# A decoder block on one core: a fourth pair of split buffers in its woven stretch, half-size raw weights, and tiles moved by 128 bytes

## The chip, the core and the metric

The kernel runs on 1 core of one Trainium2 chip. The metric is device time of one execution in microseconds (us), the median of several runs. A second, profiled execution gives the trace: engines PE (TensorE, with its weight loads as PEld), DVE (VectorE), ACT (ScalarE), POOL (GpSimd) and SP, whose queue issues most of the transfers. Times in a trace count from the first instruction; L368 is line 368 of the kernel.

## What is computed

One layer of a decoder for 256 tokens of 2048 features, in float32. The projections are split into heads, go through a sparse attention and a retention, and come together in two gated branches and an MLP:

```python
h = rms_norm(x, ln1_g[l])
proj = h @ w_in[l]
aq, ak, av, iq, ik, iw, rq, rk, rv, rg, ga, gb = jnp.split(proj, offsets, axis=-1)
...
o_attn = dsa_attention(aq, ak, av, iq, ik, iw, topk)
...
y_ret = retention_chunkwise(rq, rk, rv, log_gamma)
o_ret = jax.nn.silu(rg) * group_norm_heads(y_ret, ret_gn_g[l], ret_gn_b[l])
merged = jax.nn.sigmoid(ga) * (o_attn @ w_up_attn[l]) + jax.nn.sigmoid(gb) * (o_ret @ w_up_ret[l])
x = x + merged @ w_out[l]
h2 = rms_norm(x, ln2_g[l])
x = x + jnp.square(jax.nn.relu(h2 @ w_ff1[l])) @ w_ff2[l]
```

## The kernel before

Every large product is made of three products in a reduced-precision type. A raw weight tile (128 partitions, KC = 4 slices of 512 columns, 1 MB) is loaded by SP; half of it (HC = 2 slices) is an **item**. For each item `split_now` has ACT write the high part `whi` (L367) and DVE the low part `wlo` = raw - whi (L368). TensorE then makes three products per slice and 128 tokens: high times high, high times low, low times high (L420 to L422). The activations are split in the same way; they are the stationary operands: `act` (the normed input hT, and oT of the attention), later `xf`.

The list `program()` holds all items in the order in which TensorE uses them. `weights` takes the next item, and `ahead` first emits what lies before it: loads of items up to LOAD_AHEAD = 8 further on, as far as `room` allows, and splits of items up to SPLIT_AHEAD = 2 further on. The pairs `whi`, `wlo` come from the pool `wp`, three of each. So the split of item i+3 writes over the pair of item i, and waits until TensorE has done with it. In the last part of the kernel (from L911 on) a pool `f1` holds a fourth pair, for every item whose number leaves 3 by 4, and splits then go three items ahead.

The **woven stretch** is the list `gates()`. It weaves two kinds of items. *Quarter items* belong to the two gates GA and GB, four units in all; each unit is a Strassen-like scheme of 7 products with 4 items each, and a quarter item has 2 slices for 128 tokens, so 6 products, which go to one of three PSUM banks `pq`. Some of these products use sums of two quarter tiles, which DVE adds in place (`total`, L357, put behind the split of an item that GATE_SUMS names); for these products TensorE's stationary operands are `act` for three of the seven and forms `hx` for four. The forms are differences of the normed input's quarters, made by ACT and DVE at the start of the stretch (`h_forms`, L717 to L732). *Plain items* belong to ten ordinary blocks (`BESIDE`: the rest of RV, UA, RQ, RK); each has 2 slices for 256 tokens, so 12 products, into banks `pm`. 112 quarter items and 80 plain ones alternate, about 7 to 5: two plain items never follow each other, two quarter items sometimes do. In this stretch splits are emitted with a higher priority than the rest (L344), and a scheduler orders each engine's instructions by it.

Raw tiles of quarter items lie in a ring of six (four in `rp`, two in the pool `cx`). Raw tiles of plain items lie in `rawc`, a ring of two whole tiles in the pool `px` (L757, L313); a tile may be requested when both halves of the tile two before it are split (`room`, L377). SP's queue issues the loads in order, each waiting for the instruction that frees its place.

Pools with `side="right"` are laid out from the top of each partition downwards, one below the other: `rp`, `sp` (with n_sm = 25 small buffers of 32 bytes), `px`, then `ep` or `cx`. `hx`, 32 KB per partition, lies at the bottom of `cx`.

Of the kernel before, what the change touches and what calls it, by code (L numbers as in the profile page):

```python
# [10 lines left out]
F32 = mybir.dt.float32  # L11
# [6 lines left out]
P = 128  # L18
# [4 lines left out]
BN = 512  # L23
# [9 lines left out]
KC, HC = 4, 2  # L33
FG = 8
NG = DFF // (FG * P)
# [90 lines left out]
BESIDE = [("RV", 2), ("RV", 3)] + [("UA", i) for i in range(4)] + [(z, i) for z in ("RQ", "RK") for i in range(2)]  # L126
# [20 lines left out]
def program():  # L147

    out = [(z, h, s) for h in range(DK // KC) for s in range(KC // HC) for z in (("AK", 0), ("I", 0))]
    for key in [("I", 1), ("I", 2), ("AV", 0)] + [("AQ", i) for i in range(4)] + [("RV", 0), ("RV", 1)]:  # L150
        out += block(key)
    out += gates()
    for i in range(4):
        out += block(("RG", i))
    out += [(z, h, s) for h in range(DK // KC) for s in range(KC // HC) for z in (("UR", 0), ("UR", 1))]
    for key in [("UR", 2), ("UR", 3)] + [("O", i) for i in range(4)] + [("F1", i) for i in (1, 0)]:
        out += block(key)
    for g in range(1, NG):
        out += merged(g)
    return out + [("F2", NG - 1, i, h, s) for i in range(D // BN) for h in F2_HALVES for s in range(KC // HC)]  # L160
# [17 lines left out]
def block_kernel(ctx, tc, cst, rot, xt, gains, w, x, ret_gn_g, ret_gn_b, out):  # L178
# [5 lines left out]
    wp = ctx.enter_context(tc.tile_pool(name="wp", bufs=1))  # L184
    rp = ctx.enter_context(tc.tile_pool(name="rp", bufs=1, side="right"))
    sp = ctx.enter_context(tc.tile_pool(name="sp", bufs=1, side="right"))
    px = ctx.enter_context(tc.tile_pool(name="px", bufs=1, side="right"))
    ap = [ctx.enter_context(tc.tile_pool(name="a0", bufs=1)), tc.alloc_tile_pool(name="a1", bufs=1, reuse_waits="tile")]
    ep = tc.alloc_tile_pool(name="ep", bufs=1, side="right", reuse_waits="tile")
    dp = ctx.enter_context(tc.tile_pool(name="dp", bufs=1, space=bass.MemoryType.DRAM))  # L190
    W_NORM, W_SOFT, W_GN = 3, 5, 7
    n_stg, n_mid, n_sm = 8, 11, 25
    uid = [0]
    late = {"mid": ep}

    def nm(s):
        uid[0] += 1
        return f"{s}_{uid[0]}"
# [65 lines left out]

    at, B, off = {}, {}, 0
    for key, name, _, nk, _, n in stream():
        B[key] = (nk, n)
        for h in range(nk // KC):  # L270
            at[key, h] = (w[off:off + KC * P * n].rearrange("(p c n) -> p c n", p=P, c=KC), n)
            off += KC * P * n
    use = program()

    def tile_of(item):
        if item[0] == "Q":
            return (PRODUCTS[ORDER[item[2]]][1], item[1], item[3]), 0
        if item[0] == "F2":
            return item[:4], 0
        return item[0], item[1]  # L280

    def sum_of(item):

# [14 lines left out]
    raws, parts = {}, {}  # L298
    next_load, next_split, now, quarter, second_w, n_second = [0], [0], [0], [0], [0], [0]

    def ring(key):
        return key in BESIDE or (key[0] == "F2" and key[1] < NG - 1)

    LOAD_AHEAD, SPLIT_AHEAD, AHEAD = 8, 2, 60
    HT = KC // HC

    XROWS = (3, 5, 6, 7)

    def load(i):
        key = loads[i]  # L310
        src, n = at[key]
        if ring(key[0]):
            r = raws[key] = late["rawc"][:, second_w[0] % 2]  # L313
            second_w[0] += 1
        else:
            pool, tag, bufs = rp, "raw", 4
            if key[0][0] in QUARTERS:
                quarter[0] += 1
                if (quarter[0] - 1) % 6 >= 4:
                    pool, tag, bufs = late["f2"], "rawb", 2  # L320
            r = raws[key] = pool.tile([P, KC, BN], F32, tag=tag, name=nm("raw"), bufs=bufs)
        if i >= 2 * DK // KC:
            nc.sync.dma_start(r[:, :, :n], src)
        elif i % 2:

            for c0, c in ((0, 1), (1, 1), (2, 2)) if i == 1 else ((0, 2), (2, 2)):
                k = i // 2 * KC + c0
                nc.sync.dma_start(xts[:, k:k + c, :], xt[:, k:k + c, :])
                for z in loads[i - 1:i + 1]:
                    src, n = at[z]  # L330
                    if (i, z, c) != (1, key, 1):
                        nc.sync.dma_start(raws[z][:, c0:c0 + c, :n], src[:, c0:c0 + c, :])
                    elif c0:
                        nc.sync.dma_start(raws[z][:, :2, :n], src[:, :2, :])
        if i in XROWS:
            for j, z in list(enumerate(xsb))[XROWS.index(i) * 2:][:2]:
                nc.sync.dma_start(z, x[j // 4 * P:(j // 4 + 1) * P, j % 4 * BN:(j % 4 + 1) * BN])

    first_gate = use.index(("Q", GATES[0], 0, 0, 0))
    last_gate = len(use) - 1 - use[::-1].index(("Q", GATES[-1], len(ORDER) - 1, HK // KC - 1, HT - 1))  # L340

    def split(i):
        if first_gate - 16 <= i <= last_gate:
            with tc.high_priority(offset=AHEAD):  # L344
                split_now(i)
        else:
            split_now(i)

    def split_now(i):
        item = use[i]  # L350
        key, h = tile_of(item), item[-1]
        raw, n = raws[key], at[key][1]
        early = sum_of(item) and item[1] not in GATES

        def total():
            one, two = (raws[z] for z in sum_of(item))
            nc.vector.tensor_tensor(one, one, two, op=ALU.add)  # L357

        if early:
            total()  # L360
        pool, bufs = (late["f1"], 1) if "f1" in late and i % 4 == 3 else (wp, 3)
        hi = pool.tile([P, HC, BN], F32R, tag="whi", name=nm("whi"), bufs=bufs)
        lo = pool.tile([P, HC, BN], F32R, tag="wlo", name=nm("wlo"), bufs=bufs)
        for c0, nk in ((0, 1), (1, 1)) if i < 4 else ((0, HC),):
            src = raw[:, h * HC + c0:h * HC + c0 + nk, :n]
            a, b = hi[:, c0:c0 + nk, :n], lo[:, c0:c0 + nk, :n]
            nc.scalar.activation(a, src, AF.Copy)  # L367
            nc.vector.tensor_tensor(b, src, a.bitcast(F32), op=ALU.subtract)  # L368
        if sum_of(item) and not early:
            total()  # L370
        parts[i] = (hi, lo)

    def room(i):
        key = loads[i][0]
        if key[0] in QUARTERS and "f2" not in late:
            return False
        return not ring(key) or ("rawc" in late and second_w[0] - n_second[0] // HT < 2)  # L377

    def ahead(i):
        for _ in range(2):  # L380
            while next_load[0] < len(loads) and first_use[next_load[0]] <= i + LOAD_AHEAD and room(next_load[0]):
                load(next_load[0])
                next_load[0] += 1
            while next_split[0] < min(len(use), i + SPLIT_AHEAD + ("f1" in late) + 1):
                n_second[0] += ring(tile_of(use[next_split[0]])[0])
                split(next_split[0])
                next_split[0] += 1

# [270 lines left out]
    def strassen(item):  # L659
# [11 lines left out]
        for c in range(HC):  # L671
            products([b[to]], (ws[0][:, c], ws[1][:, c]), [form(PRODUCTS[p][0], h * KC + s * HC + c)], own and c == 0,
                     (h, s, c) == (HK // KC - 1, HT - 1, HC - 1), True)
        if (h, s) != (HK // KC - 1, HT - 1):
            return
# [68 lines left out]
    for i in range(2):  # L744
        ps = run_block(("RV", i), of(hT))
        for t in range(T):
            keep("rv", t, i, evicted(ps[t], t))
        if i == 0:
            drain()
            deal(pm=4, pq=3, pt=1)  # L750
            ep.release()
            cx = late["f2"] = tc.alloc_tile_pool(name="cx", bufs=1, side="right", reuse_waits="tile")
            hx = cx.tile([P, 2, 4, HK, P], F32R, tag="hx", name="hx")
            raw = [cx.tile([P, HK, S], F32, tag="rawb", name=nm("xr"), bufs=2) for _ in range(2)]
            for j, z in enumerate(raw):
                nc.sync.dma_start(z, xt[:, j * HK:(j + 1) * HK, :])
            late["rawc"] = px.tile([P, 2, KC, BN], F32, tag="big2", name="rawc")  # L757
            work.append(h_forms(raw))
    drain()

# [37 lines left out]
                work.append(rotated(evicted(ps[t], t), t, int(key == "RK"), i, rkT if key == "RK" else rqT))  # L798

    cx.release()  # L800
    del late["f2"], late["rawc"]
    deal(pm=4, pt=2, pa=2)
    ap[1] = tc.alloc_tile_pool(name="a2", bufs=1, reuse_waits="tile")
    rT = act_pair(1)
# [1 line left out]
    n_mid = 7  # L806
# [216 lines left out]
    def second(item):  # L1023
# [11 lines left out]
        order = [(c, slice(0, T)) for c in range(HC)]  # L1035
        if (g, i, h, s) == (NG - 1, D // BN - 1, F2_HALVES[-1], HT - 1):
            order = [(c, slice(t, t + 1)) for t in range(T) for c in range(HC)]
        for c, tt in order:
            k = h * KC + s * HC + c
            products(ps[tt], (ws[0][:, c], ws[1][:, c]), [of(hid)(g % 2 * FG + k, t) for t in range(T)][tt],  # L1040
                     (h, s, c) == (F2_HALVES[0], 0, 0), (h, s, c) == (F2_HALVES[-1], HT - 1, HC - 1))
        if (h, s) == (F2_HALVES[-1], HT - 1):
# [58 lines left out]
```

## Time and profile before

| What | Value |
|---|---|
| Median of 3 runs | 1631.78 us (1631.16 to 1632.28) |
| The profiled execution | 1630.73 us |
| Its span, first to last instruction | 1629.0 us |
| Granted TensorE clock | 1.000 |
| PE, DVE, ACT busy in the span | 1616.6, 1268.6, 1000.1 us |
| Bytes moved by the DMA engines | 353.88 MB |
| The woven stretch on PE | from 272.98 to 658.47 us |

In a row of a timeline the columns are start in us, duration in us, engine, line, operation, output and inputs, sizes; a bracket gives the engine's idle time before it and what ended it. In a row of waits they are who waited for whom, us in total, how often, and the longest. Rows that group instructions end with busy us, mean ns of one, and the idle time before them. A row of a window has its stretch, its length, then for PE, PEld, DVE, ACT and POOL the busy us and the number of instructions, then the granted clock, the share of the DMA engines and GB/s. A product's duration in the trace (0.39 us) overlaps the next one; the distance from start to start is its cost.

### The profile page before, as it was taken

How to read it: one execution, taken by the hardware profiler on the slowest of the kernel's cores; microseconds unless marked ns; L12 is line 12 of the kernel's file. 1: busy time of each engine (PE TensorE's matmuls, PEld its weight loads, DVE VectorE, ACT ScalarE, POOL GpSimd, SP SyncE). 2: the span in 40 equal slices, each digit the busy share in tenths (PEclk: the TensorE clock that was granted, in tenths of full speed). 3: DMA queues.
4: the chain of work that ended last, by engine and by line, in shares of the span. 5: the costliest groups of instructions: out<-in, count | busy, mean ns of one | idle time of the engine just before them, and what ended most of it. 6: DMA issues, size and time to landing. Idle time of an engine off the chain costs nothing.

```text
span 1629.0 us, 19406 instructions
## 1 busy us (share of the span) xinstructions
PE 1616.6 (99%) x7366; PEld 1330.7 (82%) x7366; DVE 1268.6 (78%) x1307; ACT 1000.1 (61%) x1238; POOL 100.4 (6%) x141
## 2 busy tenths in 40 slices
PE   9999999999999999999999999999999999999998
PEld 8977787777778877888888878888888888888887
DVE  6577676978787998677765488898989898989884
ACT  7555567565566666444444576667767676767672
POOL 0000000000000000010100000000000000000000
PEclk9999999999999999999999999999999999999999
DMA  9635337665666744754777564767677777777583
GB/s 332 220 140 181 130 141 272 248 225 186 229 235 259 256 176 165 254 171 174 255 251 261 193 246 164 252 212 237 220 232 233 232 233 232 233 222 230 169 252 135
DMA packets 68206, 353.88 MB, mean 217 GB/s; under 512 B 7696, under 2 KB 14480, under 8 KB 31888
## 3 DMA queue, kind: packets, MB, share of 16 engines
q1 hardware_dynamic: 51616, 311.32, 51.7%
q0 software_dynamic: 13760, 35.14, 9.8%
q10 hardware_dynamic: 2736, 6.18, 1.0%
q8 instruction: 58, 0.95, 0.2%
q14 instruction: 36, 0.29, 0.1%
HBM read 325.34 MB, written 27.26 MB: 216 GB/s over the span
## 4 chain that ended last, share of the span: by engine, by line
PE 92%; DVE 4%; ACT 2%; issue 1%; DMA 0%; POOL 0%; DVEq 0%; POOLq 0%; ACTq 0%
PE pm L421 14%; PE pm L422 14%; PE pm L420 14%; PE pq L421 8%; PE pq L422 8%; PE pq L420 8%; PE pf L420 7%; PE pf L422 7%; PE pf L421 7%; DVE wlo L368 2%; PE pt L449 1%; ACT whi L367 1%; DVE raw L357 1%; PE pa L647 1%; PE pa L620 1%
## 5 line engine op out<-in xcount | busy, mean ns | idle before, releaser
L368 DVE TENSOR_TENSOR wlo<-raw,whi 128x1024 fp32r<-128x1024 f32 (+2 forms) x528 | 627.5, 1200 | 244.9 <-ACT whi L367 238.5
L367 ACT ACTIVATE whi<-raw 128x1024 fp32r<-128x1024 f32 (+2 forms) x528 | 546.9, 1042 | 403.1 <-PE pm L422 262.7
L420 PE MATMUL pm<-whi,act 128*128 128x512 f32 (+1 forms) x1056 | 414.4, 395 | 2.4 <-ACT whi L367 2.4
L421 PE MATMUL pm<-wlo,act 128*128 128x512 f32 (+1 forms) x1056 | 407.3, 386 | 2.0 <-DVE wlo L368 2.0
L422 PE MATMUL pm<-whi,act 128*128 128x512 f32 (+1 forms) x1056 | 407.3, 386 | 0.0
L368 DVE TENSOR_TENSOR wlo<-rawc,whi 128x1024 fp32r<-128x1024 f32 x192 | 234.5, 1221 | 50.9 <-ACT whi L367 49.3
L367 ACT ACTIVATE whi<-rawc 128x1024 fp32r<-128x1024 f32 x192 | 203.5, 1060 | 103.1 <-PE pm L422 44.4
L421 PEld LDWEIGHTS pm<-wlo,act 128*128 128x128 f32 x1056 | 198.5, 188 | 43.6 <-DVE wlo L368 6.1
L420 PEld LDWEIGHTS pm<-whi,act 128*128 128x128 f32 x1056 | 198.4, 188 | 43.4 <-ACT whi L367 4.6
L422 PEld LDWEIGHTS pm<-whi,act 128*128 128x128 f32 x1056 | 198.3, 188 | 37.7
L357 DVE TENSOR_TENSOR raw<-raw,raw 128x2048 f32<-128x2048 f32 x88 | 201.2, 2286 | 0.8
L420 PE MATMUL pf<-whi,act 128*128 128x512 f32 x512 | 200.0, 391 | 0.0
L421 PE MATMUL pf<-wlo,act 128*128 128x512 f32 x512 | 199.4, 389 | 0.0
L422 PE MATMUL pf<-whi,act 128*128 128x512 f32 x512 | 199.4, 389 | 0.0
L420 PE MATMUL pq<-whi,xf 128*128 128x512 f32 x392 | 154.3, 394 | 0.0
L422 PE MATMUL pq<-whi,xf 128*128 128x512 f32 x392 | 152.7, 390 | 0.0
L421 PE MATMUL pq<-wlo,xf 128*128 128x512 f32 x392 | 152.6, 389 | 0.0
L422 PEld LDWEIGHTS pf<-whi,act 128*128 128x128 f32 x512 | 96.1, 188 | 20.1
L420 PEld LDWEIGHTS pf<-whi,act 128*128 128x128 f32 x512 | 96.0, 188 | 20.0 <-ACT whi L367 0.4
L421 PEld LDWEIGHTS pf<-wlo,act 128*128 128x128 f32 x512 | 96.2, 188 | 19.8
L422 PEld LDWEIGHTS pq<-whi,xf 128*128 128x128 f32 x392 | 73.6, 188 | 15.5
L421 PEld LDWEIGHTS pq<-wlo,xf 128*128 128x128 f32 x392 | 73.7, 188 | 14.7
(166 smaller groups left out, 1419.9 us busy)
## 6 DMA issues: line engine op xcount, KB each, us to landing
raw<-in_w_dram SPq DMA_DIRECT2D x180, 1024.0 KB, 5.8
rawc<-in_w_dram SPq DMA_DIRECT2D x96, 1024.0 KB, 5.5
sums<-ev POOLq DMA_DIRECT2D x56, 256.0 KB, 5.4
raw<-in_w_dram SPq DMA_DIRECT2D x8, 736.0 KB, 4.6
raw<-in_w_dram SPq DMA_DIRECT2D x7, 512.0 KB, 7.4
raw<-in_w_dram SPq DMA_DIRECT2D x8, 368.0 KB, 7.7
stg<-in_x_dram SPq DMA_DIRECT2D x8, 256.0 KB, 7.5
rv<-stg POOLq DMA_DIRECT2D x8, 256.0 KB, 4.6
```

Source lines behind the costliest of these rows:

```text
L357: nc.vector.tensor_tensor(one, one, two, op=ALU.add)
L367: nc.scalar.activation(a, src, AF.Copy)
L368: nc.vector.tensor_tensor(b, src, a.bitcast(F32), op=ALU.subtract)
L420: nc.tensor.matmul(d, h, hi, start=first, stop=False, skip_group_check=skip)
L421: nc.tensor.matmul(d, h, lo, start=False, stop=False, skip_group_check=skip)
L422: nc.tensor.matmul(d, l, hi, start=False, stop=last, skip_group_check=skip)
L449: nc.tensor.transpose(ps[:, c * P:(c + 1) * P], src[:, c * P:(c + 1) * P], ident)
L620: nc.tensor.matmul(ps[:, a * n:(a + 1) * n], qT[:, h0 + a, :], kT[:, j, :n], start=True, stop=True)
L647: nc.tensor.matmul(po, vv[:, c, j * HD:(j + 1) * HD], pT, start=(c == 0), stop=(c == t))
```

## The change

Four things are changed, all for the woven stretch.

- The pool `cx` gets a fourth pair `whi`, `wlo`, used for every item whose number leaves 3 by 4, and in the stretch splits go three items ahead.
- Raw weights of plain items are loaded in halves of 512 KB, one for each item, into a ring of three halves, which now lies in `cx`.
- The pool `px` is released before the stretch and made anew behind it (as `px2`), so that `cx` may use its place.
- n_sm grows from 25 to 29. The four small buffers more take 128 bytes, and all pools of the right side below them begin 128 bytes lower.

```diff
-    px = ctx.enter_context(tc.tile_pool(name="px", bufs=1, side="right"))
+    px = tc.alloc_tile_pool(name="px", bufs=1, side="right", reuse_waits="tile")
...
-    n_stg, n_mid, n_sm = 8, 11, 25
+    n_stg, n_mid, n_sm = 8, 11, 29
...
-            at[key, h] = (w[off:off + KC * P * n].rearrange("(p c n) -> p c n", p=P, c=KC), n)
+            src = w[off:off + KC * P * n].rearrange("(p c n) -> p c n", p=P, c=KC)
+            if key in BESIDE:
+                for i in range(HT):
+                    at[key, h, i] = (src[:, i * HC:(i + 1) * HC], n)
+            else:
+                at[key, h] = (src, n)
...
-        return item[0], item[1]
+        return item if item[0] in BESIDE else item[:2]
...
     def ring(key):
-        return key in BESIDE or (key[0] == "F2" and key[1] < NG - 1)
+        if key in BESIDE:
+            return 3
+        return 2 if key[0] == "F2" and key[1] < NG - 1 else 0
...
-            r = raws[key] = late["rawc"][:, second_w[0] % 2]
+            r = raws[key] = late["rawc"][:, second_w[0] % ring(key[0])]
...
-        key, h = tile_of(item), item[-1]
+        key, h = tile_of(item), 0 if item[0] in BESIDE else item[-1]
...
         pool, bufs = (late["f1"], 1) if "f1" in late and i % 4 == 3 else (wp, 3)
+        if "fourth" in late and i % 4 == 3:
+            pool, bufs = late["fourth"], 1
...
-        return not ring(key) or ("rawc" in late and second_w[0] - n_second[0] // HT < 2)
+        n = ring(key)
+        return not n or ("rawc" in late and second_w[0] - (n_second[0] // HT if key[0] == "F2" else n_second[0]) < n)
...
-            while next_split[0] < min(len(use), i + SPLIT_AHEAD + ("f1" in late) + 1):
-                n_second[0] += ring(tile_of(use[next_split[0]])[0])
+            while next_split[0] < min(len(use), i + SPLIT_AHEAD + ("f1" in late or "fourth" in late) + 1):
+                n_second[0] += ring(tile_of(use[next_split[0]])[0]) > 0
...
             ep.release()
+            px.release()
...
-            late["rawc"] = px.tile([P, 2, KC, BN], F32, tag="big2", name="rawc")
+            late["rawc"] = cx.tile([P, 3, HC, BN], F32, tag="rawc", name="rawc")
+            late["fourth"] = cx
...
-    del late["f2"], late["rawc"]
+    del late["f2"], late["rawc"], late["fourth"]
+    second_w[0] = n_second[0] = 0
+    px = ctx.enter_context(tc.tile_pool(name="px2", bufs=1, side="right", reuse_waits="tile"))
```

The change moves instructions on ACT, DVE, PE and SP. In the rows below a name's last number only tells tiles apart; `raw` are quarter tiles, `rawc` the ring of plain ones, `xr` and `hx` the forms at the stretch's start. The lines L367, L368, L357, L727 and L730 become L376, L377, L364, L737 and L740.

The first place is the start of the stretch on DVE, where the forms begin. Before:

```order
265 L368 TENSOR_TENSOR wlo_445_2387<-raw_409_2185,whi_444_2386 128x1024
266 L727 TENSOR_TENSOR xr_428_2273<-xr_427_2272,xr_428_2273 128x8x128
267 L727 TENSOR_TENSOR xr_427_2272<-xr_427_2272 128x8x128
268 L368 TENSOR_TENSOR wlo_447_2406<-raw_431_2279,whi_446_2405 128x1024
269 L730 TENSOR_TENSOR hx_2271<-xr_428_2273,hx_2271 128x1024
270 L368 TENSOR_TENSOR wlo_449_2425<-rawc_2276,whi_448_2424 128x1024
```

And in the changed program:

```order
265 L377 TENSOR_TENSOR wlo_445_2373<-raw_409_2185,whi_444_2372 128x1024
266 L377 TENSOR_TENSOR wlo_447_2393<-raw_431_2280,whi_446_2392 128x1024
267 L737 TENSOR_TENSOR xr_428_2274<-xr_427_2273,xr_428_2274 128x8x128
268 L737 TENSOR_TENSOR xr_427_2273<-xr_427_2273 128x8x128
269 L377 TENSOR_TENSOR wlo_449_2412<-rawc_2277,whi_448_2411 128x1024
270 L740 TENSOR_TENSOR hx_2272<-xr_428_2274,hx_2272 128x1024
```

The first split of the quarter tile raw_431 stood behind the first two instructions of the forms; now it stands ahead of them, and so does every split behind it, by one.

The second place is DVE in the third unit of the stretch, around the add that the trace of before has at 478.34 us. Before:

```order
404 L368 TENSOR_TENSOR wlo_709_3865<-raw_684_3739,whi_708_3864 128x1024
405 L368 TENSOR_TENSOR wlo_711_3875<-raw_674_3686,whi_710_3874 128x1024
406 L357 TENSOR_TENSOR raw_684_3739<-raw_684_3739,raw_699_3816 128x2048
407 L368 TENSOR_TENSOR wlo_714_3893<-rawc_2276,whi_713_3892 128x1024
408 L368 TENSOR_TENSOR wlo_717_3906<-raw_674_3686,whi_716_3905 128x1024
```

And in the changed program:

```order
405 L377 TENSOR_TENSOR wlo_711_3892<-raw_676_3712,whi_710_3891 128x1024
406 L377 TENSOR_TENSOR wlo_713_3903<-rawc_2277,whi_712_3902 128x1024
407 L364 TENSOR_TENSOR raw_686_3765<-raw_686_3765,raw_701_3843 128x2048
408 L377 TENSOR_TENSOR wlo_716_3921<-raw_676_3712,whi_715_3920 128x1024
409 L377 TENSOR_TENSOR wlo_719_3935<-rawc_2277,whi_718_3934 128x1024
```

The split of the plain item (wlo_714 before, wlo_713 now) stood behind the add of two quarter tiles and now stands ahead of it.

The third place is the same one on PE: the products of that plain item and of the next quarter item. Before:

```order
2031 L420 MATMUL pm_702_3822<-whi_713_3892,act_175_1071 128x512
2032 L420 MATMUL pm_703_3823<-whi_713_3892,act_175_1071 128x512
2033 L420 MATMUL pq_718_3910<-whi_716_3905,hx_2271 128x512
2034 L421 MATMUL pm_702_3822<-wlo_714_3893,act_175_1071 128x512
2035 L422 MATMUL pm_702_3822<-whi_713_3892,act_175_1071 128x512
```

And in the changed program:

```order
2031 L430 MATMUL pm_704_3850<-whi_712_3902,act_175_1071 128x512
2032 L431 MATMUL pm_704_3850<-wlo_713_3903,act_175_1071 128x512
2033 L432 MATMUL pm_704_3850<-whi_712_3902,act_175_1071 128x512
2034 L430 MATMUL pm_705_3851<-whi_712_3902,act_175_1071 128x512
2035 L431 MATMUL pm_705_3851<-wlo_713_3903,act_175_1071 128x512
```

Before, three products that need only a high part were drawn ahead of the first that needs the low part; now the item's products stand in their plain order.

More of the change, by code (lines that the diff above doesn't have):

```diff
@@ L263, in block_kernel @@
     nc.scalar.activation(wout, warm[:, :8], AF.Copy)
+    HT = KC // HC
     at, B, off = {}, {}, 0
@@ L301, in ring @@
     def ring(key):
-        return key in BESIDE or (key[0] == "F2" and key[1] < NG - 1)
+        if key in BESIDE:
+            return 3
+        return 2 if key[0] == "F2" and key[1] < NG - 1 else 0
     LOAD_AHEAD, SPLIT_AHEAD, AHEAD = 8, 2, 60
-    HT = KC // HC
     XROWS = (3, 5, 6, 7)
```

## The prediction

> **What bounds the kernel now.** I read the page first (busy shares and the chain that ended last), then the stretch that the change touches, by window, waits and timeline.
>
> ```profile
> PE 1616.6 (99%) x7366; PEld 1330.7 (82%) x7366; DVE 1268.6 (78%) x1307; ACT 1000.1 (61%) x1238; POOL 100.4 (6%) x141
> ...
> PE 92%; DVE 4%; ACT 2%; issue 1%; DMA 0%; POOL 0%; DVEq 0%; POOLq 0%; ACTq 0%
> ```
>
> TensorE is busy in 99% of the span and carries 92% of the chain; whatever is to be won is time in which it stands or runs below its pace. The 6% of DVE and ACT in the chain are the places to look at. What the pace is, and how long the woven stretch takes, three rows of PE's timeline tell: the stretch's first product, one of 25 that follow each other undisturbed, and the first product behind the stretch.
>
> ```profile
> 272.98 0.39 PE L420 MATMUL pq<-whi,act 128*128 128x512 f32 x1
> ...
> 653.03 0.39 PE L420 MATMUL pq<-whi,act 128*128 128x512 f32 x1
> ...
> 658.47 0.39 PE L420 MATMUL pm<-whi,act 128*128 128x512 f32 x1
> ```
>
> From 653.03 to 658.47 lie 24 products: 5.44 / 24 = 0.2267 us each, the undisturbed pace. The stretch lasts 658.47 - 272.98 = 385.5 us. By the code it holds 112 quarter items of 6 products and 80 plain items of 12, so 1632 products, and the transposes of the rotated queries and keys. Four of these take 0.44 us in the chain's list, and 24 lie in the stretch (x24 for L714 there).
>
> ```profile
> 557.33 0.44 PE pt L714 x4
> 272.90:658.50 385.60, 380.72 (x1659) 307.34 (x1658) 325.42 (x275) 234.80 (x250) 18.88 (x35) 1.00 0.59 217
> ```
>
> 1632 x 0.2267 + 24 x 0.11 = 372.6 us. **So 12.9 us of the stretch are lost, and that is all that this change can win there.** The window's row says what they are not: the granted clock is 1.00, the DMA engines are used to 0.59, DVE to 325 of 386 us, ACT to 235.
>
> Where the 12.9 us are: PE's waits inside the stretch are ten.
>
> ```profile
> PE pm L420 <- ACT whi L367: 1.9, 4, 0.5
> PE pm L421 <- DVE wlo L368: 1.3, 3, 0.6
> PE pq L420 <- ACT whi L367: 1.2, 2, 0.9
> PE pq L421 <- DVE wlo L368: 0.5, 1, 0.5
> ```
>
> 1.9 + 1.3 + 1.2 + 0.5 = 4.9 us, all for the split of a weight (whi from ACT, wlo from DVE), none for a transfer. One of them in full, with DVE and ACT around it:
>
> ```profile
> 480.91 0.40 PE L420 MATMUL pq<-whi,hx 128*128 128x512 f32 x1
> 481.82 0.50 PE L421 MATMUL pm<-wlo,act 128*128 128x512 f32 x1 [0.50 <-DVE wlo L368]
> 482.16 0.39 PE L422 MATMUL pm<-whi,act 128*128 128x512 f32 x1
> ...
> 478.34 2.28 DVE L357 TENSOR_TENSOR raw<-raw,raw 128x2048 f32<-128x2048 f32 x1
> 480.54 1.22 DVE L368 TENSOR_TENSOR wlo<-rawc,whi 128x1024 fp32r<-128x1024 f32 x1
> ...
> 479.25 1.06 ACT L367 ACTIVATE whi<-raw 128x1024 fp32r<-128x1024 f32 x1 [0.30 <-PE pq L422]
> 480.70 1.05 ACT L367 ACTIVATE whi<-rawc 128x1024 fp32r<-128x1024 f32 x1
> ```
>
> DVE is in an add of two quarter tiles (2.20 us from start to start) while PE needs the low part of a plain item. ACT had been held until 479.25 by PE, which still held the pair of buffers (the bracket). The halt costs more than its bracket of 0.50: 481.82 - 480.91 = 0.91 instead of 0.23 is 0.68, and the product behind it takes 0.34 instead of 0.23, 0.11 more. Ten halts: 4.9 + 10 x (0.18 + 0.11) = **7.8 us**.
>
> The other loss is pace. The starts of two quarter items on hx, of a plain item behind them and of the next on hx, and then of two quarter items on act and of what follows; from start to start lie 12 products each:
>
> ```profile
> 334.44 0.40 PE L420 MATMUL pq<-whi,hx 128*128 128x512 f32 x1
> ...
> 337.24 0.40 PE L420 MATMUL pm<-whi,act 128*128 128x512 f32 x1
> ...
> 339.99 0.40 PE L420 MATMUL pq<-whi,hx 128*128 128x512 f32 x1
> ...
> 344.11 0.39 PE L420 MATMUL pq<-whi,act 128*128 128x512 f32 x1
> ...
> 346.83 0.62 PE L420 MATMUL pm<-whi,act 128*128 128x512 f32 x2
> ```
>
> 12 products on hx take 337.24 - 334.44 = 2.80 us, 12 on act in the same kind of bank 346.83 - 344.11 = 2.72; the plain item straight behind hx takes 339.99 - 337.24 = 2.75. The groups say the same of all of them: mean 398 against 390 ns.
>
> ```profile
> L420 PE MATMUL pq<-whi,hx 128*128 128x512 f32 x128 | 50.9, 398 | 0.9 <-ACT whi L367 0.9
> L420 PE MATMUL pq<-whi,act 128*128 128x512 f32 x96 | 37.5, 390 | 0.3 <-ACT whi L367 0.3
> ```
>
> 3 x 128 products on hx x 0.08 / 12 = 2.6 us, and the plain items behind them, some 46 (64 quarter items on hx, 5 of 7 followed by a plain one) x 0.03 = 1.4: **4.0 us**. 7.8 + 4.0 = 11.8 of the 12.9; 1.1 us I assign to nothing.
>
> **The change part by part.** *Fourth pair, three items ahead.* No instruction is added; each of the 192 splits may start one item earlier. With three pairs the split of item i+3 waits until PE is done with item i, and must be ready after items i+1 and i+2: at the least two quarter items, 12 products, 2.72 us. The split itself is 1.06 + 1.22 = 2.28 us, so any 0.5 us in front of it on ACT or DVE halts PE, and an add is 2.20. With four pairs three items lie between, at the least two quarters and a plain one, 24 products, 5.44 us, against 2.28 + 2.20 + an eviction of 0.6 = 5.1. In the order of the changed program the plain item's split of 480.54 stands ahead of the add, as the second place above shows. So eight of the ten halts go; they ask for 0.35 to 0.73 us each and get 2.7 more.
>
> The first two, at the stretch's start, are another matter:
>
> ```profile
> 292.26 0.62 PE L420 MATMUL pm<-whi,act 128*128 128x512 f32 x2
> 293.81 0.50 PE L420 MATMUL pq<-whi,hx 128*128 128x512 f32 x1 [0.93 <-ACT whi L367]
> ...
> 296.21 0.39 PE L422 MATMUL pm<-whi,act 128*128 128x512 f32 x1
> 297.11 0.50 PE L421 MATMUL pq<-wlo,hx 128*128 128x512 f32 x1 [0.52 <-DVE wlo L368]
> ...
> 266.39 1.23 DVE L368 TENSOR_TENSOR wlo<-raw,whi 128x1024 fp32r<-128x1024 f32 x1 [1.72 <-ACT whi L367]
> ...
> 267.53:297.06 29.53, 29.50 (x25) 1.00 0.58 222
> ```
>
> DVE is busy in 29.50 of these 29.53 us: it makes the forms hx beside the splits, and there the lookahead is used up. Before 267.53 it had gaps of 1.3 to 1.8 us in front of each split (one is the bracket at 266.39). The fourth pair moves exactly one split, 1.14 us from start to start, into such a gap (the first place above: the first split of raw_431 now stands ahead of the forms). The first row holds two products, the second of them at 292.49. The two halts come to (293.81 - 292.49 - 0.23) + (297.11 - 296.21 - 0.23) = 1.09 + 0.67 = 1.76 us; 1.14 earlier leaves about 0.6, with its tail 0.7. **Gain of the halts: 7.8 - 0.7 = 7.1 us.** Bounds: nothing of it (0) if DVE's backlog grows with PE's pace, 7.8 if the start's halts go too.
>
> *The right side by 128 bytes.* In the built program hx begins at byte 113856 of a partition, remainder 192 by 256; act (43072 and 75840), xf, whi and wlo all leave 64. After the change hx begins at 109632 and leaves 64. Among the stationary tiles of the long products hx alone leaves 192, and hx alone runs slow, at 0.2333 us. xf and the second act overlap hx's range of addresses and are not slow, so the range is not it. I take the 4.0 us as won; bounds 0 and 4.0. The Trainium skill, page "SBUF — State Buffer", section "Who interferes with whom", says that only the port pair shared by VectorE and GpSimd causes contention, and "PE and ACT never wait on anyone": by that rule an address cannot slow a product, and the gain here would be 0. The trace has a slower pace on hx that this rule does not name; which is right the changed kernel shows, and the rule is the first rival's. Other tiles move by the same 128 bytes. The short products of attention and retention and the transposes read some; at hx's 6.7 ns each some 450 of them would give up to 3.0 us. I take 0, since no row shows them slow by address. The fourth pair lies at 171072 and 175168, remainder 64: 0, and at the worst hx's 6.7 ns on a quarter of 1632 products, 2.7 us lost.
>
> *Halves in a ring of three.* 80 loads of 512 KB for 40 of 1 MB, the same bytes, 40 more issues on SP.
>
> ```profile
> rawc<-in_w_dram SPq DMA_DIRECT2D x38, 1024.0 KB, 5.4
> DMA to landing us min/median/max: 4.7/5.4/9.7
> L367 ACT ACTIVATE whi<-rawc 128x1024 fp32r<-128x1024 f32 x79 | 83.8, 1061 | 56.4 <-PE pm L422 44.4 <-PE pq L422 11.8
> ```
>
> A half's place comes free at the split of the third half before it, three plain and 4.2 quarter items earlier: 3 x 2.72 + 4.2 x 1.36 = 13.9 us. In that time SP issues it (0.33), it lands (5.4 for twice its size, 9.7 the longest) and ACT reads it (1.06): 6.8 us, 11.1 at the worst. Before, the first half of a tile had the same distance. Its row lists only PE as what ACT waited for, no transfer. SP's requests wait for DVE instructions in ascending order in the changed program, so none stands behind a later one. Cost 0, cover 2.8 us and more; without it ACT, first in, stands and PE with it.
>
> **Sum.** 7.1 + 4.0 = 11.1 us. From the profiled execution's 1630.73 us (span 1629.0 and 1.7 around it): 1619.6. It stood 1.05 below the median of the three runs, 1631.78, so I forecast 1620.7 as the median.
>
> **Rivals.** *The pace on hx stays* (it is its place among the products or the rule above, not its address): 1631.78 - 7.1 = 1624.7. For it: the cause is read from one tile. Against: products on act in the same banks. *DVE is the bound behind the halts*: from 469 to 483 it has no gap, and the deeper lookahead only moves the halts; half of them stay, and hx stays slow: 1631.78 - 3.6 = 1628.2. Against: 88% of the shorter stretch, and four items' cushion. *The fourth pair changes nothing*, because each fourth split waits for something else: 1631.8. *Slower: the halves land late.* Place: ACT in front of the split of a plain half, with the next quarter splits and the evictions behind it. It decides from a landing of 13.9 - 0.33 - 1.06 = 12.5 us; each 0.2 us beyond costs 80 x 0.2 = 16, so a landing of 12.7 us gives 1620.7 + 16 = 1636.7. Against: 9.7 is the longest seen here, of twice the size.
>
> **How the numbers follow.** Forecast 0.56, hx stays slow 0.24, half the halts stay 0.10, nothing 0.06, slower 0.04. The range reaches from 1618, which takes in the unassigned 1.1 and part of the other tiles' gain, to 1627.5, which leaves out most of the third case and the last two. Faster by over 0.2% (3.3 us; about what a measurement of this kernel can tell from no change) holds the first two and half of the third: 0.85. Within 0.2%: 0.11. Slower: 0.04.
>
> **What would show it.** The stretch from the first product on act in a pq bank to the first behind it: 374.4 us for 385.5. PE's waits in it for whi and wlo: one or two, near its start, for 4.9 us in ten. The hx groups at a mean of 390 for 398 ns; if they stay at 398 the first rival holds. ACT's waits for PE in front of whi grow. If ACT waits for rawc's transfer, the last rival is at work; if PE waits for an eviction, something that I priced at nothing. Outside the stretch nothing should move by over 1 us; if it does, the 128 bytes did it and I was wrong to take 0.

## The result, and the profile after

The changed kernel takes 1619.61 us (median of 4 runs, 1619.32 to 1619.91), the kernel before 1631.47 beside it (1631.02 to 1632.28). The ratio is 0.9927, with a 95% interval from 0.991 to 0.9944: 11.9 us faster, where 1620.7 us and 11.1 us were forecast. The profiled executions say the same: spans of 1629.0 and 1618.0 us.

The page of the changed kernel, in the lines that were read first before (busy shares, and the chain that ended last):

```profile
span 1618.0 us, 19499 instructions
PE 1609.8 (99%) x7366; PEld 1331.7 (82%) x7366; DVE 1267.2 (78%) x1307; ACT 1000.6 (62%) x1238; POOL 100.6 (6%) x141
PE 95%; DVE 2%; ACT 1%; DMA 1%; issue 1%; POOL 0%; DVEq 0%; ACTq 0%; POOLq 0%
```

TensorE was the bound and still is. DVE and ACT together have 3% of the chain, of 6% before. PE's timeline of the changed kernel, with the stretch's first product and the first product behind it, and all of PE's waits between them (a row names who waited for whom, us in total, times, longest):

```profile
273.06 0.39 PE L430 MATMUL pq<-whi,act 128*128 128x512 f32 x1
...
647.51 0.39 PE L430 MATMUL pm<-whi,act 128*128 128x512 f32 x1
...
PE pq L430 <- ACT whi L376: 0.5, 1, 0.5
```

The stretch takes 647.51 - 273.06 = 374.45 us; it took 385.5 and was forecast at 374.4. Of the waits of before, 4.9 us in ten, one of 0.5 us is left. And the pace, in the groups of the changed kernel (busy us and mean ns of one stand behind the bar):

```profile
L430 PE MATMUL pq<-whi,hx 128*128 128x512 f32 x128 | 50.1, 391 | 0.5 <-ACT whi L376 0.5
L430 PE MATMUL pq<-whi,act 128*128 128x512 f32 x96 | 37.3, 389 | 0.0
```

398 ns have become 391 on hx, beside 389 on act. Why a halt is gone, the plain item shows that had to wait at 481.82 before. Here are PE's first product with its low part in the changed kernel, and DVE around it:

```profile
474.38 0.39 PE L431 MATMUL pm<-wlo,act 128*128 128x512 f32 x1
...
470.95 1.22 DVE L377 TENSOR_TENSOR wlo<-rawc,whi 128x1024 fp32r<-128x1024 f32 x1
472.09 2.28 DVE L364 TENSOR_TENSOR raw<-raw,raw 128x2048 f32<-128x2048 f32 x1
```

The split now runs ahead of the add and ends at 472.17, 2.2 us before PE asks for it. DVE does the same work as before, the urgent thing first; its busy time is the third in the window's row of the whole stretch (PE, PEld, DVE, ACT, POOL), 324.78 us where the prediction's row has 325.42:

```profile
272.90:647.50 374.60, 374.08 (x1658) 308.31 (x1657) 324.78 (x275) 235.38 (x250) 16.79 (x31) 1.00 0.63 223
```

The start of the stretch is the place where the forecast left something:

```profile
293.20 0.50 PE L430 MATMUL pq<-whi,hx 128*128 128x512 f32 x1 [0.49 <-ACT whi L376]
293.54 0.40 PE L431 MATMUL pm<-wlo,act 128*128 128x512 f32 x1
293.78 0.40 PE L432 MATMUL pm<-whi,act 128*128 128x512 f32 x1
294.02 0.40 PE L431 MATMUL pm<-wlo,act 128*128 128x512 f32 x1
```

One halt of 0.49 us; the first product behind it takes 0.34 us from start to start and the next ones 0.24 instead of 0.2267, although nothing is waited for. By the eleventh the pace is back: beyond the first one's 0.11 us this tail is 0.06 us in all. A second halt, at 296.1 us, of 0.18 us, shows in PE's starts alone. At the first one PE waits for ACT, but ACT had itself been held by an add of DVE:

```profile
292.09 2.01 ACT L376 ACTIVATE whi<-raw 128x1024 fp32r<-128x1024 f32 x2 [3.64 <-DVE raw L364]
```

To compare kernels I split each stretch's loss by PE's starts: where the next product starts over 0.26 us later, what exceeds 0.2266 is called **halts**, so the first product behind a halt counts there too; what the other products exceed it by is called **slow products**. Products beside the transposes bring some 0.5 us of halts in every kernel. (The transposes themselves, 2.3 to 2.7 us, are the rest of a stretch's length above 369.8.) All numbers in us; "beside" is the kernel before, in the runs made together with each.

| Kernel | median | beside | stretch | halts | slow products |
|---|---|---|---|---|---|
| before | 1631.47 | | 385.5 | 9.3 | 4.1 |
| changed | 1619.61 | 1631.47 | 374.5 | 1.6 | 0.4 |
| e1: 128 bytes alone | 1628.76 | 1631.65 | 383.4 | 10.1 | 1.0 |
| e4: hx alone by 128 bytes | 1629.24 | 1631.65 | 383.3 | 10.1 | 1.0 |
| e2: changed without the 128 bytes | 1624.24 | 1631.65 | 378.3 | 1.5 | 4.5 |
| e3: changed without the fourth pair | 1629.04 | 1631.65 | 383.3 | 10.0 | 1.1 |
| e7: changed, all at remainder 192 | 1620.63 | 1631.56 | 374.1 | 1.2 | 0.4 |
| e5: changed, hx 64 bytes lower | 1620.47 | 1631.56 | 374.8 | 1.2 | 1.2 |
| e6: changed, hx 192 bytes lower | 1623.11 | 1631.56 | 377.4 | 1.1 | 4.0 |
| e8: changed, hx 256 bytes lower | 1619.57 | 1631.56 | 374.0 | 1.2 | 0.4 |
| e11: changed, fourth pair at 192 | 1622.13 | 1631.32 | 376.9 | 1.4 | 3.1 |
| e10: changed, one form by POOL | 1621.00 | 1631.32 | 376.1 | 3.2 | 0.4 |
| e9: changed, F1's splits first | 1621.59 | 1631.32 | 374.1 | 1.3 | 0.3 |
| e12: changed, scalings by DVE | 1618.57 | 1630.74 | 373.3 | 0.5 | 0.3 |

### The profile page after: what moved, and what is told of

It is laid out like the page before. It is cut to its first block, busy times and chain, and to the rows that moved or that the text cites. A ratio compares the mean times of both kernels' runs of the same rounds, so it can differ in the third digit from the quotient of the medians.

```text
span 1618.0 us, 19499 instructions
## 1 busy us (share of the span) xinstructions
PE 1609.8 (99%) x7366; PEld 1331.7 (82%) x7366; DVE 1267.2 (78%) x1307; ACT 1000.6 (62%) x1238; POOL 100.6 (6%) x141
## 4 chain that ended last, share of the span: by engine, by line
PE 95%; DVE 2%; ACT 1%; DMA 1%; issue 1%; POOL 0%; DVEq 0%; ACTq 0%; POOLq 0%
PE pm L431 14%; PE pm L432 14%; PE pm L430 14%; PE pq L430 8%; PE pq L431 8%; PE pq L432 8%; PE pf L430 7%; PE pf L432 7%; PE pf L431 7%; PE pt L459 1%; DVE wlo L377 1%; PE pa L630 1%; PE pa L842 1%; PE pa L657 1%; DMA xr<-in_xt_dram 0%
## 5 line engine op out<-in xcount | busy, mean ns | idle before, releaser
L377 DVE TENSOR_TENSOR wlo<-raw,whi 128x1024 fp32r<-128x1024 f32 (+2 forms) x528 | 628.6, 1199 | 252.4 <-ACT whi L376 243.6
L376 ACT ACTIVATE whi<-raw 128x1024 fp32r<-128x1024 f32 (+2 forms) x528 | 546.9, 1042 | 418.4 <-PE pm L432 274.9
L377 DVE TENSOR_TENSOR wlo<-rawc,whi 128x1024 fp32r<-128x1024 f32 x192 | 234.1, 1219 | 35.3 <-ACT whi L376 31.6
L376 ACT ACTIVATE whi<-rawc 128x1024 fp32r<-128x1024 f32 x192 | 203.5, 1060 | 82.0 <-PE pq L432 23.7
L364 DVE TENSOR_TENSOR raw<-raw,raw 128x2048 f32<-128x2048 f32 x88 | 201.0, 2284 | 0.6
```

## The experiments

### The terms one by one

**The 128 bytes alone** (e1), on the kernel before:

```diff
-    n_stg, n_mid, n_sm = 8, 11, 25
+    n_stg, n_mid, n_sm = 8, 11, 29
```

> The kernel before with n_sm = 29 alone: every tile of the right side below sp lies 128 bytes lower, hx at byte 113728 (remainder 64 by 256). Theory (the address of hx sets its pace): 4.0 us faster than before, about 1627.5; hx groups at a mean of 390 ns; the ten halts for whi and wlo stay at 4.9 us in the waits. Rival (the pace on hx comes from its place among the products or from the halts): no change, 1631.5, hx groups at 398 ns.

Measured 1628.76, 2.9 us faster than before (ratio 0.998, 0.9971 to 0.9989). Its hx group and PE's waits in the stretch:

```profile
L420 PE MATMUL pq<-whi,hx 128*128 128x512 f32 x128 | 50.0, 391 | 1.0 <-ACT whi L367 1.0
...
PE pm L420 <- ACT whi L367: 2.0, 4, 0.5
PE pm L421 <- DVE wlo L368: 1.4, 3, 0.6
PE pq L420 <- ACT whi L367: 1.3, 2, 1.0
PE pq L421 <- DVE wlo L368: 0.5, 1, 0.5
```

The pace on hx is mended by nothing but an address, so the rival of "place among the products" falls. The gain is smaller than 4.0, and the waits say why: 5.2 us for 4.9. PE arrives sooner at splits that come no sooner. By the table slow products fall by 3.1 us (4.1 to 1.0) and halts take 0.8 of it back.

**hx alone** (e4), on the kernel before; the pad moves no other tile:

```diff
             hx = cx.tile([P, 2, 4, HK, P], F32R, tag="hx", name="hx")
+            cx.tile([P, 32], F32, tag="pad", name="pad")
```

> The kernel before with a pad of 128 bytes behind hx in its pool, so that hx alone moves, to byte 113728 (remainder 64 by 256), and every other tile stays. Theory (hx's own address): the same as with all tiles moved, 4.0 us faster, 1627.5, hx groups at 390 ns. Rival (another tile of the right side that moves with n_sm, such as the raw tiles that ACT and DVE read): no change, 1631.5. Rival (place among the products): no change, 1631.5.

Measured 1629.24 (0.9985, 0.9976 to 0.9994), with the same stretch as e1, 383.3 us, and its hx group at 391 ns. It is hx's own address; the other tiles that n_sm moves give nothing.

**The changed kernel without the 128 bytes** (e2):

```diff
-    n_stg, n_mid, n_sm = 8, 11, 29
+    n_stg, n_mid, n_sm = 8, 11, 25
```

> The changed kernel with n_sm = 25: the fourth pair, three items ahead and the halves stay, but hx lies at byte 109760 and the fourth pair at 171200 and 175296, all with remainder 192 by 256. Theory (address of hx, as the stationary operand): 4.0 us slower than the changed kernel, 1623.6, hx groups at 398 ns; products of act with the fourth pair stay at 0.2267 us. If the moving operand's address counts too, a quarter of the 1632 products loses 6.7 ns each, 2.7 us more: 1626.3. Rival (the pace on hx was a consequence of the halts): 1619.6, hx groups at 390 ns.

Measured 1624.24 (0.9955, 0.9942 to 0.9967): 7.4 us faster than before, 4.6 slower than the changed kernel. Its hx group and PE's only wait in the stretch:

```profile
L430 PE MATMUL pq<-whi,hx 128*128 128x512 f32 x128 | 50.9, 397 | 0.4 <-ACT whi L376 0.4
...
PE pq L430 <- ACT whi L376: 0.4, 1, 0.4
```

The halts are gone and the slow pace is there: the two losses have separate causes. But in this trace it is not only hx that is slow. Products of act with the fourth pair, which here lies at remainder 192, have a mean of 232.4 ns from start to start, and products of hx with the fourth pair, both at 192, a median of 227. So 528 products of the stretch have unequal remainders here, 264 on hx and 264 on act, where the kernel before has 384, all on hx. That did not fit the rule of the prediction and led to e7, e11 and the others below.

**The changed kernel without the fourth pair** (e3); splits go two items ahead again, halves, ring and 128 bytes stay:

```diff
-            late["fourth"] = cx
...
-    del late["f2"], late["rawc"], late["fourth"]
+    del late["f2"], late["rawc"]
```

> The changed kernel without the fourth pair and with splits two items ahead in the stretch; halves, ring of three and the 128 bytes stay (hx at 117824, remainder 64). Theory (the fourth pair and three items ahead end the halts, the halves cost and win nothing): 7.1 us slower than the changed kernel, 1626.7, with some ten halts and 4.9 us of waits in the stretch. Rival (the halves' ring, whose loads no longer wait for two splits of a tile, ends part of the halts): half of them gone, 1623. Rival (the halves land late without the deeper lookahead, or cost something): above 1628.

Measured 1629.04 (0.9984, 0.9976 to 0.9993), 9.4 us slower than the changed kernel where 7.1 was expected. PE's waits in its stretch:

```profile
PE pm L430 <- ACT whi L376: 2.0, 4, 0.5
PE pm L431 <- DVE wlo L377: 1.4, 3, 0.6
PE pq L430 <- ACT whi L376: 1.3, 2, 1.0
PE pq L431 <- DVE wlo L377: 0.5, 1, 0.5
```

They are e1's, row by row, and so are the stretch (383.3 for 383.4) and the median (1629.04 for 1628.76). The two kernels differ by the halves and their ring, so these cost and win nothing that can be seen; the fourth pair with the third item ahead, which were not run apart, is what ends the halts. Why it is worth more than 7.1 is told below.

### What rule the addresses follow

The prediction read: a stationary tile at remainder 192 by 256 is slow. In the kernel before, whi, wlo and act all lie at 64, so this could as well be a rule on the *difference* of the two operands. **Everything at 192** (e7) tells them apart:

```diff
-    n_stg, n_mid, n_sm = 8, 11, 29
+    n_stg, n_mid, n_sm = 8, 11, 25
...
     wp = ctx.enter_context(tc.tile_pool(name="wp", bufs=1))
+    wp.tile([P, 32], F32, tag="pad", name="pad")
```

> The changed kernel with n_sm = 25 and a pad of 128 bytes at the start of wp: whi, wlo, act, xf, hx and the fourth pair all lie at remainder 192 by 256. Theory as the prediction put it (a tile at remainder 192 is slow, at 64 it is not): all long products run at 0.2325 us or so, 5.8 ns more on 1632 products in the stretch, 9.5 us, and as much on the other 5100 or so, about 39 us in all: 1658. Theory now (what decides is whether the stationary and the moving operand leave the same remainder, as in the trace without the shift, where hx at 192 with the fourth pair at 192 has a median of 227 ns from start to start): all alike, so as fast as the changed kernel, 1619.6, pq groups on hx and act both at 390 ns.

Measured 1620.63 (1618.53 to 1621.98; 0.9925, 0.9913 to 0.9938), where the prediction's rule asked for 1658. Its hx group:

```profile
L431 PE MATMUL pq<-whi,hx 128*128 128x512 f32 x128 | 50.1, 391 | 0.1
```

So 192 is as good as 64, if both operands have it. The stretch is as short as the changed kernel's (374.1); the median's 1.0 us more lies outside it, where the traces of these kernels differ by up to 2 us among themselves (1243.2 to 1245.2, e9 apart), and no run explains it.

**The fourth pair alone at 192** (e11), the moving operand, with hx kept at 64 by a second pad:

```diff
         lo = pool.tile([P, HC, BN], F32R, tag="wlo", name=nm("wlo"), bufs=bufs)
+        if pool is late.get("fourth") and not padded:
+            padded.append(pool.tile([P, 32], F32, tag="pad", name="pad"))
...
             hx = cx.tile([P, 2, 4, HK, P], F32R, tag="hx", name="hx")
+            cx.tile([P, 32], F32, tag="pad0", name="pad0")
```

> The changed kernel with a pad of 128 bytes above hx's and the raw tiles' place, so that the fourth pair lies at 170944 and 175040 (remainder 192 by 256), and a second pad of 128 bytes that brings hx to 109376 (remainder 64). Theory (both operands must leave the same remainder): the quarter of the products that uses the fourth pair, 408, runs 5.8 ns slower, 2.4 us, and the products behind them lose about as much again as in the kernel without the shift: 1622 to 1623.6, and products with the other three pairs stay at 227 ns. Rival (only the stationary operand's address counts, as the prediction took it): 1619.6.

Measured 1622.13 (0.9943, 0.993 to 0.9957), 2.5 us slower than the changed kernel. The moving operand counts as the stationary one does.

**Other distances of hx** (e5, e6, e8), on the changed kernel, with a pad of 64, 192 or 256 bytes behind hx:

```diff
             hx = cx.tile([P, 2, 4, HK, P], F32R, tag="hx", name="hx")
+            cx.tile([P, 16], F32, tag="pad", name="pad")
```

> The changed kernel with a pad of 64 bytes behind hx: hx at 109568 (remainder 0 by 256), all else as it was (moving operands at 64). Theory a (the remainders by 256 must be equal): slower by what the shift brought, some 4 us, 1623.9, hx groups above 390 ns. Theory b (both must lie in the same half of 256 bytes): as fast as the changed kernel, 1619.6, hx groups at 390 ns.

> The changed kernel with a pad of 192 bytes behind hx: hx at 109440 (remainder 128 by 256), moving operands at 64. Theories a and b: hx in the other half of 256 bytes, slow, 1623.9. Theory c (only a distance of exactly 128 bytes by 256 is slow): 1619.6.

> The changed kernel with a pad of 256 bytes behind hx: hx at 109376 (remainder 64 by 256, but 320 by 512, where the moving operands leave 64). Theory (the remainder by 256 decides): no change, 1619.6, hx groups at 390 ns. Rival (the remainder by 512 decides): slow, about 1624.

Measured 1620.47, 1623.11 and 1619.57 (0.9926, 0.9941 and 0.9923, each some 0.0013 either way). Two group rows, of e6 and of e8:

```profile
L430 PE MATMUL pq<-whi,hx 128*128 128x512 f32 x128 | 50.9, 398 | 0.0
...
L430 PE MATMUL pq<-whi,hx 128*128 128x512 f32 x128 | 50.1, 391 | 0.0
```

A move by 256 bytes changes nothing, so the rule goes by 256. One by 192 (hx at 128) costs 3.5 us against e8, as theories a and b had it. One by 64 (hx at 0) lies between: its products are slowed, but the stretch only by 0.7 us against e8's, and neither theory had that. Joining each product with its two operands' places gives the whole picture, the mean distance from start to start between products of the same kind, distances over 0.3 us left out:

```text
moving  stationary   mean ns   products   kernel
  64        64        226.9      1616     changed
 192       192        226.9      1616     e7
  64       192        232.9       321     before
 192        64        232.7       334     e11
  64       128        233.7       331     e6
  64         0        229.3       331     e5
```

### What is left at the start, and one step beyond

**One form by POOL** (e10), on the changed kernel:

```diff
-            nc.vector.tensor_tensor(lo, d, hi.bitcast(F32), op=ALU.subtract)
+            (nc.gpsimd if f == G7 else nc.vector).tensor_tensor(lo, d, hi.bitcast(F32), op=ALU.subtract)
```

> The changed kernel, but the low part of the form G7 (one of the four L740 at the start of the stretch, 1.14 us of DVE) is made by POOL. Theory (the two halts left at 292.3 and 296.1 us are DVE's backlog, in which every instruction since 267 counts): with 1.14 us less of it the waits of 0.49 and 0.02 us go, about 1.0 us with their tails, 1618.6. Rival (the halts there hang on ACT or on the raw tiles' loads): the waits stay, 1619.6. Rival (POOL's work slows DVE's instructions beside it): the waits grow, 1620 or more.

Measured 1621.00 (0.9935, 0.9923 to 0.9948): the last rival. In its timeline POOL's subtraction, and DVE's split beside it:

```profile
271.98 3.37 POOL L740 TENSOR_TENSOR hx<-xr,hx 128x1024 fp32r<-128x1024 f32 x1 [21.00 <-ACT hx L738]
...
272.99 3.44 DVE L377 TENSOR_TENSOR wlo<-raw,whi 128x1024 fp32r<-128x1024 f32 x1
...
PE pm L431 <- DVE wlo L377: 1.0, 1, 1.0
PE pq L431 <- DVE wlo L377: 0.7, 2, 0.3
```

DVE's split took 3.44 us for 1.22 and ended 1.1 us behind POOL's subtraction, as if it had begun only when that was done. So DVE won 1.14 us and lost 2.22; its backlog grew by 1.1 us, and PE's waits from 0.5 to 1.7. The edit missed its aim, but it shows what it was made for, with the sign turned round: 1.1 us more on DVE between 267 and 297 us made the stretch 1.7 us longer. The Trainium skill, page "SBUF — State Buffer", section "Who interferes with whom", says that VectorE and GpSimd share a pair of ports under an exclusive lock, and that a two-input operation of VectorE contends with GpSimd's reads; the 3.44 us agree.

**Scalings by DVE** (e12), on the changed kernel: 6 of the 16 scalings ahead of the forms go from ACT to DVE, into gaps that DVE has before 267 us, so that the forms begin earlier.

```diff
-                nc.scalar.activation(z, z, AF.Copy, scale=g)
+                if j and k >= 2:
+                    nc.vector.tensor_scalar(z, z, g, None, op0=ALU.mult)
+                else:
+                    nc.scalar.activation(z, z, AF.Copy, scale=g)
```

> The changed kernel, but 6 of the 16 scalings of xr at the start of the stretch (L732, 0.42 us each on ACT) are made by DVE, in gaps that DVE has before 267 us, so that the forms start some 2.5 us earlier. Theory (the two halts left at 292.3 and 296.1 are DVE's backlog from 267 to 297; POOL's attempt added 1.1 us to it and lengthened the halts): 2 us less of backlog ends both halts, 0.49 us of waits and some 1.1 with what hangs on them: 1618.5. Rival (the halts hang on something else, or the scalings hold up the splits of before): 1619.6 or more.

Measured 1618.57 beside 1630.74 (0.9924, 0.991 to 0.9937). DVE's rows of the scalings, the second group straight behind a split, and the first of the forms, which was at 268.06:

```profile
260.52 0.88 DVE L733 TENSOR_SCALAR xr<-xr,gT 128x256 f32<-128x256 f32 x3 [1.03 <-DMA xr<-in_xt_dram]
...
262.45 0.87 DVE L733 TENSOR_SCALAR xr<-xr,gT 128x256 f32<-128x256 f32 x3
...
264.90 1.22 DVE L740 TENSOR_TENSOR xr<-xr,xr 128x1024 f32<-128x1024 f32 x1
```

The forms start 3.2 us earlier, PE has no wait in the stretch at all, and the stretch is 373.3 us, 1.15 shorter. That is shown by the trace. ACT has less to do as well, but in the changed kernel it was DVE's add that ACT waited for ahead of the halt (the row at 292.09). The median is 1.04 us below the changed kernel's, but the kernel before was 0.7 us quicker beside it too, so in the ratio (0.9924 for 0.9927) the step can't be told from none. It is the best version measured, by the trace and by a hair.

**F1's splits first** (e9), on the changed kernel. Behind the stretch two halts are left at 928.6 and 929.8 us, for splits queued behind the second norm's work on ACT.

```diff
-        if first_gate - 16 <= i <= last_gate:
+        if first_gate - 16 <= i <= last_gate or first_f1 <= i < first_f1 + 16:
```

> The changed kernel, but the splits of the 16 items from the first of F1 on are emitted with the stretch's priority too; in ACT's order two of them move ahead of the scaling for the second norm. Theory (the halts at 928.6 and 929.8 us, 0.52 and 0.53 us of waits for a split queued behind that scaling on ACT, are of the same kind as those of the stretch): they go, 1.0 us with 0.3 each of tails, 1618.0. Rival (the scaling, now later, makes TensorE wait for the normed input instead): no change or slower, 1619.6 to 1621.

Measured 1621.59 (1619.69 to 1622.39; 0.9936, 0.9923 to 0.9948). In the trace the two halts stand where they stood. What moved ahead are two splits of the norm's second half, at 941 and 944 us, which nobody waited for. I had taken their place in the order for the first half's. Behind them the forms of xf slid back, and one new wait stands behind these, for the evictions at 963 us:

```profile
PE pt L460 <- ACT stg L1016: 1.4, 1, 1.4
```

So this run says nothing on the halts at 929. The new wait of 1.4 us is all that the trace shows of the priority; that it comes from the later forms is read from the order alone, and in the ratio (0.9936 for 0.9927) the run can't be told from the changed kernel.

## Why the prediction was right, step by step

- **The bound and what can be won.** The 12.9 us that it gave the change to win are down to 374.45 - 372.6 = 1.9, and outside the stretch nothing moved: the span less the stretch is 1243.5 us before, 1243.6 now. Right.
- **Halts, 7.1 us.** Eight of ten went, at the places named, and by the mechanism named: the split of 480.54 stands ahead of its add. In the table halts fell by 7.7 us (9.3 to 1.6). The price of a halt was right: the ten of before, with the product behind each, come to 7.6 us in PE's starts for the 7.8 of the forecast. The start kept 1.06 us (0.65 + 0.18, and 0.11 behind each) for the 0.7 forecast, and e10 and e12 show that DVE's backlog is the reason given. What the step left out are five smaller halts, 0.29 to 0.37 us from start to start (at 281.4, 403.9, 452.0, 499.4 and 645.0 us), which PE's rows of waits don't list (in the rows of its weight loads whi and wlo are waited for 17 times). With the products behind them they come to 0.95 us, and they went too: nearly the 1.1 us that were "assigned to nothing". The tails behind halts are small, some 0.05 us each: e1, with no unequal remainders and some 15 halts more than the changed kernel, has 0.6 us more of slow products.
- **Pace, 4.0 us.** Slow products fell by 3.7 us (4.1 to 0.4), 2.2 on hx and 1.5 on act. The forecast had 2.6 on hx and 1.4 on what follows it. Of the 1.5 some 0.6 are tails of halts that went: the address alone is worth 3.1 (e1), so this term was too high.
- **The sum, 11.1 us.** The stretch is 11.0 shorter, and that the forecast is so near is in part luck: what a term brings depends on which is taken first, and the sum didn't say so. With the 128 bytes first, the stretch loses 2.1 us (385.5 to 383.4, e1) where 4.0 were forecast, and then the fourth pair with the halves 8.9 (383.3 in e3 to 374.5) where 7.1 were; the two errors cancel. With the fourth pair first it loses 7.2 (e2) and then 3.8. Of the 1.7 us between the two orders some 1.0 comes from the fourth pair itself, which without the 128 bytes lies at 192: from e2 to the changed kernel slow products fall by 4.1 us, for 528 products with unequal remainders, and by 3.1 from the kernel before to e1, for 384. The rest is that a faster pace is partly waited away while PE halts for splits: halts grow by 0.8 us in e1, and by 0.1 from e2 to the changed kernel.
- **The rule on addresses** failed as it was put, and did no harm: "Among the stationary tiles of the long products hx alone leaves 192, and hx alone runs slow" was true, but 192 is not slow in itself (e7). What counts is that both operands leave the same remainder by 256. With this, "the fourth pair lies at remainder 64: 0" is right for a better reason, and its bound of 2.7 us if it didn't was near: e11 has 2.5.
- **The first rival** fell with e4. The rule that stood for it, "PE and ACT never wait on anyone" (the Trainium skill, page "SBUF — State Buffer", section "Who interferes with whom"), isn't borne out here for the pace of products, as the prediction read it: with hx alone moved (e4), products on hx follow each other at 227.0 ns for 232.9. The measurement decides. The rival on DVE as the bound fell too: DVE is as busy as before, 324.8 of 374.6 us, and PE waits once.
- **Halves, cost 0.** e3 beside e1 shows it. The longest landing in the changed kernel stays under the 12.5 us from which it was to decide, and nobody waited for it (rows of the ring's tile in the stretch):

```profile
DMA to landing us min/median/max: 3.1/4.0/10.6
```

- **ACT's waits for PE in front of whi "grow".** They didn't. Before and after, in the stretch:

```profile
ACT whi L367 <- PE pm L422: 100.1, 62, 2.7
ACT whi L367 <- PE pq L422: 26.0, 80, 0.9
...
ACT whi L376 <- PE pm L432: 85.0, 55, 1.7
ACT whi L376 <- PE pq L432: 26.9, 89, 0.9
```

126.1 us became 111.9: ACT's work is the same in a stretch that is 11 us shorter, so its idle time had to fall. A cushion shows in how early a split is done, not in how long its engine then waits.

## What to carry to other kernels

Where the bound engine halts for short moments behind helpers that are busy nearly nine tenths of the time, depth can be the cure: here one more buffer and one more item of lookahead ended all halts but those at the start, where the helper has no gap at all. There it helped to let the helper begin earlier (e12). Small losses on the bound engine are not independent: mending one can lengthen the waits for another, so price such terms alone and together, and look whether a run that leaves one out changes something else as well, as e2 did with the fourth pair's address. And compare the pace of the same product on different tiles: a few per cent between groups that should be equal can be an address.

## What the runs showed of the hardware

- TensorE's pace depends on where its two operands lie to each other in a partition: with equal remainders by 256 bytes 226.9 ns from start to start for a 128x512 product, with remainders 128 apart, or the stationary one 64 above the moving one (e6), 232.7 to 233.7, with the stationary one 64 below (e5) 229.3. Which bytes are read at what moment isn't seen in a trace, so the cause stays open. Only products of this form and type, and distances in steps of 64, were tried.
- Slow pairs slow the next products too: in e6 1193 products with both operands at 64 had a mean of 227.9 ns, for 226.9 in the changed kernel.
- A halt of TensorE is followed by one product at 0.33 to 0.34 us and some ten at up to 0.24 for 0.2267, with no wait in the trace: 0.11 us for the first and some 0.05 for the others together.
- A DVE subtraction that began 1.0 us behind POOL's subtraction of 3.37 us took 3.44 us instead of 1.22 (e10).
